# One core, three transformer blocks: the instruction scheduler is given a finer model of the engines

## The chip, the cores and the metric

The kernel runs on one core of one Trainium2 chip. The metric is the device time of one execution in microseconds (us); the kernel before takes 1453.17 us, the median of 3 runs. A core has a matrix engine (PE in the profile, with its weight loads as PEld), a vector engine (DVE), a scalar engine with function tables (ACT), GpSimd (POOL) and SyncE (SP), which issues the DMAs here. Each engine works through its own list of instructions strictly in the order in which the program put them there, and waits on semaphores for the others.

## The reference, cut to what matters

A sequence of 256 tokens of width 1024, in fp32, goes through two layers of a first block and one layer of a second block.

```python
def first_block(x, ...):                       # DEPTH = 2 layers
    h = rms_norm(x, norm1_g[l]); z = h @ w_in[l]
    o_a = mla_mixer(cq, ckv, kpe, ...)         # 8 heads, causal softmax attention
    o_b = gla_mixer(gq, gk, gv, glr, gr, ...)  # gated linear attention in chunks of 64
    o_c = s5_mixer(su, ...)                    # state-space scan
    g = sigmoid(gates + gate_b[l])             # three gates of width 1024
    merged = g0*(o_a @ w_br_mla[l]) + g1*(o_b @ w_br_gla[l]) + g2*(o_c @ w_br_s5[l])
    x = x + merged @ w_out[l]
    x = x + square(relu(rms_norm(x, norm2_g[l]) @ w_ff1[l])) @ w_ff2[l]

def second_block(x, ...):                      # one layer
    z = rms_norm(x, g_pre_mix) @ w_in
    y_attn = dilated_attention_mixer(q, k, v, rel_bias_table, w_attn_out)   # 24 heads in 3 groups
    y_conv = silu(layer_norm(conv31(u * sigmoid(gate)))) @ w_conv_out + b_conv_out
    merged = sigmoid(z_ga)*y_attn + sigmoid(z_gc)*y_conv
    x = x + rms_norm(merged @ w_mix_out, g_post_mix)
    x = x + rms_norm(swiglu_ffn(rms_norm(x, g_pre_ffn), ...), g_post_ffn)
```

## The kernel before, in words

All weights are read once from HBM, in 424 "units" of 128 rows by 1024 columns. For each unit SP issues a DMA into a buffer `raw`; ACT rounds it to the high part `wH` (line 160 of a helper) and DVE forms the rest `wL` (line 161). Each product is made of three matmuls, high by high, low by high and high by low: lines 169, 170 and 171 where the weights are held in the engine and 256 tokens stream past (24 matmuls for a unit), lines 175 to 177 where 512 weight columns stream past the tokens.

The mixers between the weight products are "chains": generators that emit some small PE instructions, then vector and scalar work on their results, and yield. Two chains matter most below. `mla_attn` takes two heads at a time: transposes of q and k into PSUM (line 872), the copy `mla_T` on ACT (875), scores (884, 885), mask and row minimum on DVE (888, 890), exponentials on ACT (895), normalization on DVE (897, 899) into `mla_p`, transposes (906) with their copies `mla_pT` (908), the product with v (912), and the split of the result into `moH` and `moL`, which the product with `w_br_mla` reads. `conv_ln`, the layer norm behind the convolution, sums channels (1346), centres (1359), squares on ACT (1363), sums again (1349), forms the reciprocal root on POOL, broadcasts it over the partitions with two matmuls of a diagonal `diag` (1332, 1333), multiplies (`cv`, 1375; each of two instructions takes four of eight channel blocks), applies SiLU with gain and bias (1378, eight instructions), and splits into `cH` and `cL`, which the product with `w_conv_out` (1551 to 1553) reads. `attn2`, the dilated attention of the second block, has scores (1422, 1424), bias and minimum (1426, 1428), exponentials (1436), scaling (1440), transposes (1448, copied by 1450) and the product with v (1457).

Which unit follows which, and after which unit a chain advances by a step, is written out by hand in the strings `SCHED` (one for each layer) and `SCHED2`; letters with numbers are units, the others are steps of chains. So the program is emitted in one order. Tile, the framework that it is written in, does not keep that order: when the context closes, its scheduler goes through the emitted instructions with a model of the five engines, and on each engine puts next what is ready earliest by that model and by the priorities that the program sets. What it decides is the order of the lists, and these are then fixed; on the chip nothing is reordered.

Buffers are limited: two PSUM buffers for weight products (`ps_mm`), five for chains (`ps_acc`) and one for transposes (`ps_tr`), three `raw` buffers, and four pairs of `wH` and `wL`, fetched three units ahead.

## Time and profile before

| | before |
|---|---|
| median of 3 runs | 1453.17 us (1452.96 to 1453.4) |
| profiled execution, its own time | 1451.78 us |
| its span (first to last instruction) | 1450.0 us |
| PE busy | 1402.2 us, 97% |
| PEld busy | 1272.1 us, 88% |
| DVE busy | 1012.9 us, 70% |
| ACT busy | 835.1 us, 58% |
| mean granted PE clock | 0.991 of full speed |

The profiled execution is 1.39 us under the median, and 1.78 us of it lie outside the span. A busy PE is not a PE at its peak: its matmuls are pipelined and their recorded ends overlap. The time in which PE is idle is what another order can give or take, since the instructions are the same.

### The profile page before, as it was taken

Reading aid. Unit: us, or ns where it says so; the run is one execution under the profiler, and the core shown is the slowest. Engines: PE = TensorE matmul, PEld = TensorE weight load, DVE = VectorE, ACT = ScalarE, POOL = GpSimd, SP = SyncE. Lnnn points to the kernel's source line nnn. Section 1 sums busy time; section 2 is a strip of 40 time slices with the busy share of each in tenths; the row PEclk is TensorE's granted clock in tenths of the full one; section 3 lists DMA queues with packets and bytes.
Section 4 is the critical chain, followed back from the end, with each engine's and each line's share of the span. In section 5 each row is a group of like instructions: output and inputs, shape, how many; then the busy total and the mean of one; then the engine's idle time right before and its main releaser. Section 6 shows DMA issues by size and latency. Waiting matters only on the chain.

```text
span 1450.0 us, 26147 instructions
## 1 busy us (share of the span) xinstructions
PE 1402.2 (97%) x10412; PEld 1272.1 (88%) x10412; DVE 1012.9 (70%) x1860; ACT 835.1 (58%) x1455; POOL 46.3 (3%) x51
## 2 busy tenths in 40 slices
PE   8999999999999999989999999999999999899998
PEld 6989889888899899888988999989888989689997
DVE  6987776689455667766566555579999846655555
ACT  6865566467754555455546444465678574544443
POOL 1000100000000000111000000000000000000000
PEclk9999999999999999999999999999999999999999
DMA  6622344555445552344456555565555445365553
GB/s 221 218 88 90 119 169 151 175 189 177 159 172 185 201 175 77 116 147 160 148 188 225 186 185 189 189 227 183 181 152 171 150 153 183 117 218 189 185 183 112
DMA packets 71058, 243.10 MB, mean 168 GB/s; under 512 B 7864, under 2 KB 11656, under 8 KB 70936
## 3 DMA queue, kind: packets, MB, share of 16 engines
q1 hardware_dynamic: 70936, 241.43, 48.8%
q8 instruction: 81, 1.33, 0.4%
q14 instruction: 41, 0.34, 0.1%
HBM read 237.17 MB, written 4.23 MB: 166 GB/s over the span
## 4 chain that ended last, share of the span: by engine, by line
PE 62%; DVE 13%; ACT 7%; issue 3%; DMA 2%; POOL 2%; POOLq 0%; DVEq 0%; ACTq 0%; SPq 0%
PE mm L169 11%; PE mm L171 11%; PE mm L170 11%; PE acc L175 7%; PE acc L177 7%; PE acc L176 7%; DVE wL L161 4%; ACT wH L160 2%; DVE cv L1321 2%; POOL rsq L184 2%; DMA raw<-in_wst_dram 2%; ACT sp L1436 1%; PE acc L553 1%; PE acc L1457 1%; ACT sp L1440 1%
## 5 line engine op out<-in xcount | busy, mean ns | idle before, releaser
L161 DVE TENSOR_TENSOR wL<-raw,wH 128x1024 fp32r<-128x1024 f32 (+1 forms) x410 | 496.1, 1211 | 260.4 <-ACT wH L160 259.0
L160 ACT ACTIVATE wH<-raw 128x1024 fp32r<-128x1024 f32 (+1 forms) x410 | 429.1, 1048 | 379.5 <-PE mm L170 184.7
L169 PE MATMUL mm<-hH,wH 128*128 128x256 f32 x1792 | 515.5, 288 | 5.0 <-ACT gt L1065 3.5
L171 PE MATMUL mm<-hH,wL 128*128 128x256 f32 x1792 | 510.4, 285 | 0.0
L170 PE MATMUL mm<-hL,wH 128*128 128x256 f32 x1792 | 509.7, 284 | 0.0
L169 PEld LDWEIGHTS mm<-hH,wH 128*128 128x128 f32 x1792 | 342.8, 191 | 17.2 <-issue 4.4
L170 PEld LDWEIGHTS mm<-hL,wH 128*128 128x128 f32 x1792 | 343.2, 191 | 3.6 <-issue 0.4
L171 PEld LDWEIGHTS mm<-hH,wL 128*128 128x128 f32 x1792 | 342.9, 191 | 1.4 <-issue 0.9
L175 PE MATMUL acc<-wH,fH 128*128 128x512 f32 x344 | 135.2, 393 | 0.0
L176 PE MATMUL acc<-wL,fH 128*128 128x512 f32 x344 | 134.8, 392 | 0.0
L177 PE MATMUL acc<-wH,fL 128*128 128x512 f32 x344 | 134.2, 390 | 0.6 <-DVE fL L161 0.6
L1321 DVE SCALAR_TENSOR_TENSOR cv<-u,ppt,cv 128x256 f32<-128x256 f32 x184 | 78.0, 478 | 0.3
L177 PEld LDWEIGHTS acc<-wH,fL 128*128 128x128 f32 x344 | 64.6, 188 | 15.2 <-DVE fL L161 1.1
L175 PEld LDWEIGHTS acc<-wH,fH 128*128 128x128 f32 x344 | 64.9, 189 | 11.4 <-ACT fH L160 0.2
L176 PEld LDWEIGHTS acc<-wL,fH 128*128 128x128 f32 x344 | 64.9, 189 | 10.5
L160 ACT ACTIVATE fH<-ffr 128x256 fp32r<-128x256 f32 x56 | 23.4, 417 | 68.4 <-DVE ffr L1224 68.4
L161 DVE TENSOR_TENSOR fL<-ffr,fH 128x256 fp32r<-128x256 f32 x56 | 23.7, 424 | 23.0 <-ACT fH L160 23.0
L176 PE MATMUL acc<-wL,hH 128*128 128x512 f32 x96 | 37.9, 398 | 0.9 <-DVE wL L161 0.9
L175 PE MATMUL acc<-wH,mH 128*128 128x512 f32 x96 | 37.8, 394 | 0.0
L176 PE MATMUL acc<-wL,mH 128*128 128x512 f32 x96 | 37.8, 394 | 0.0
L175 PE MATMUL acc<-wH,hH 128*128 128x512 f32 x96 | 37.8, 399 | 0.0
L177 PE MATMUL acc<-wH,hL 128*128 128x512 f32 x96 | 37.7, 396 | 0.0
(435 smaller groups left out, 2171.3 us busy)
## 6 DMA issues: line engine op xcount, KB each, us to landing
raw<-in_wst_dram SPq DMA_DIRECT2D x420, 512.0 KB, 3.5
xd<-x SPq DMA_DIRECT2D x6, 512.0 KB, 4.0
x<-xd SPq DMA_DIRECT2D x6, 512.0 KB, 5.7
bias<-bdram SPq DMA_DIRECT2D x8, 384.0 KB, 6.2
gnorm<-in_rows_dram SPq DMA_DIRECT2D x3, 512.0 KB, 5.3
raw<-in_wst_dram SPq DMA_DIRECT2D x4, 384.0 KB, 3.5
x<-in_x_dram SPq DMA_DIRECT2D x4, 256.0 KB, 4.5
x<-in_x_dram SPq DMA_DIRECT2D x2, 512.0 KB, 5.2
```

What stands on the lines that cost most here:

```text
L160: nc.scalar.activation(H, src, AF.Copy)
L161: nc.vector.tensor_sub(L, src, H)
L169: nc.tensor.matmul(ps, H[:, w], aH[:, i, :], start=(i == 0), stop=False)
L170: nc.tensor.matmul(ps, H[:, w], aL[:, i, :], start=False, stop=False)
L171: nc.tensor.matmul(ps, L[:, w], aH[:, i, :], start=False, stop=(i == nk - 1))
L175: nc.tensor.matmul(ps, aH[:, ki, tt], H[:, cols], start=start, stop=False)
L176: nc.tensor.matmul(ps, aH[:, ki, tt], L[:, cols], start=False, stop=False)
L177: nc.tensor.matmul(ps, aL[:, ki, tt], H[:, cols], start=False, stop=stop)
L184: nc.gpsimd.tensor_tensor(o, m, k.mhalf[:, 0:1].to_broadcast([P, n]), op=OP.pow)
L553: nc.tensor.matmul(ps[:, (4 * c + q) * 64:(4 * c + q + 1) * 64], E[:, c, :], us[:, q, :], start=True, stop=True)
L1321: nc.vector.scalar_tensor_tensor(st.cv[:, ct], u(ct, i), w(ct, i), st.cv[:, ct], op0=OP.mult, op1=OP.add)
L1436: nc.scalar.activation(s[i][:, :, cs], s[i][:, :, cs], AF.Exp, scale=-1.0, bias=mj[:, b:b + 1], accum_out=sm[:, b:b + 1])
```

## The change

One argument of the Tile context is set. The scheduler then times the instructions by a finer model of the engines (one that steps through a time line of each instruction's parts) in place of the plain one. The text of the kernel, its hand-written strings and its priorities stay, and so do the instructions: 9582 on PE, 1862 on DVE, 1357 on ACT, 56 on POOL and 484 on SP before and after, with 14 loads of a function table on ACT in both.

```diff
-    with _tile.TileContext(nc) as tc:
+    with _tile.TileContext(nc, schedule_with_timeline_sim=True) as tc:
```

What moves is the place of the instructions in the lists: 5693 of the 9582 on PE, 1451 on DVE and 995 on ACT stand elsewhere, 2 on POOL and 67 on SP. Three places follow. Numbers behind a name tell its allocations apart.

PE at the end of the layer-0 `mla_attn`, its last two heads, before: `tr_3025` are the k transposes, `acc_3164` and `acc_3212` the scores of the two heads, `tr_3226` and `tr_3232` the transposes of their probabilities, and every `mm` is a weight product of 24 matmuls.

```order
L872 MATMUL tr_3025<-cst_85,mla_kn_2854 96x128
...
L171 MATMUL mm_3136<-s5oH_2241,wL_3035 128x256
L884 MATMUL acc_3164<-mla_T_3030,mla_T_3023 128x128
L885 MATMUL acc_3164<-mla_T_3030,mla_T_3023 128x256
L169 MATMUL mm_3184<-hH_187,wH_3066 128x256
...
L171 MATMUL mm_3184<-hH_187,wL_3067 128x256
L884 MATMUL acc_3212<-mla_T_3030,mla_T_3023 128x128
L885 MATMUL acc_3212<-mla_T_3030,mla_T_3023 128x256
L906 MATMUL tr_3226<-cst_85,mla_p_3171 128x128 x3
L169 MATMUL mm_3250<-hH_187,wH_3099 128x256
...
L906 MATMUL tr_3232<-cst_85,mla_p_3219 128x128
```

The same place of the changed kernel:

```order
L872 MATMUL tr_3025<-cst_85,mla_kn_2854 96x128
L884 MATMUL acc_3164<-mla_T_3030,mla_T_3023 128x128
L885 MATMUL acc_3164<-mla_T_3030,mla_T_3023 128x256
L884 MATMUL acc_3212<-mla_T_3030,mla_T_3023 128x128
L885 MATMUL acc_3212<-mla_T_3030,mla_T_3023 128x256
L906 MATMUL tr_3226<-cst_85,mla_p_3171 128x128 x3
L906 MATMUL tr_3232<-cst_85,mla_p_3219 128x128 x3
L912 MATMUL acc_3163<-mla_pT_3230,mla_v_2016 64x256
L912 MATMUL acc_3163<-mla_pT_3236,mla_v_2016 64x256
L912 MATMUL acc_3163<-mla_pT_3230,mla_v_2016 64x128
L912 MATMUL acc_3163<-mla_pT_3236,mla_v_2016 64x128
L169 MATMUL mm_3314<-moH_2017,wH_3180 128x256
```

Weight products of gates and of the S5 branch, three of them ahead of `acc_3164` and one ahead of `acc_3212`, have moved ahead of `tr_3025`, so that the steps of the chain now follow each other directly, up to the product that reads `moH`.

PE between the second broadcast of `conv_ln` (`acc_13455`) and the first product with `w_conv_out` (`mm_13691`), before; `mm_13486` to `mm_13605` are four weight products of the gates, `tr_13555` to `tr_13652` transposes of `attn2`:

```order
L1333 MATMUL acc_13455<-diag_13459,cst_85 128x128
L1424 MATMUL acc_13462<-k_12888,q_12775 128x256
L1424 MATMUL acc_13463<-k_12888,q_12775 128x256
L169 MATMUL mm_13486<-hH_10720,wH_13336 128x256
...
L171 MATMUL mm_13605<-hH_10720,wL_13483 128x256
L1457 MATMUL acc_13554<-pT2_13559,v2_0_10887 64x256
...
L1448 MATMUL tr_13646<-cst_85,sp_13320 128x128 x3
L1448 MATMUL tr_13652<-cst_85,sp_13324 128x128 x3
L1551 MATMUL mm_13691<-cH_13635,wH_13523 128x256
```

And of the changed kernel:

```order
L171 MATMUL mm_13605<-hH_10720,wL_13483 128x256
L1333 MATMUL acc_13455<-diag_13456,cst_85 128x128
L1422 MATMUL acc_13462<-k_12888,q_12775 128x128
L1422 MATMUL acc_13463<-k_12888,q_12775 128x128
L1424 MATMUL acc_13462<-k_12888,q_12775 128x256
L1424 MATMUL acc_13463<-k_12888,q_12775 128x256
L1333 MATMUL acc_13455<-diag_13459,cst_85 128x128
L1551 MATMUL mm_13691<-cH_13635,wH_13523 128x256
L1551 MATMUL mm_13725<-cH_13635,wH_13569 128x256
L1448 MATMUL tr_13555<-cst_85,sp_13320 128x128
L1552 MATMUL mm_13691<-cL_13637,wH_13523 128x256
```

The four gate products now stand ahead of the broadcast, and the transposes of `attn2` behind the first rows of the product with `w_conv_out`.

ACT at the same place, before; the rows on `cv` are SiLU, those of line 1436 exponentials, of 1440 the scaling of `attn2`:

```order
L1378 ACT_TABLE_LOAD
L1378 ACTIVATE cv_11475<-cv_11475,ppt_86 128x256
L1436 ACT_TABLE_LOAD
L1436 ACTIVATE sp_13320,asm_13474<-sp_13320,amj_13472 128x3x128
...
L1378 ACT_TABLE_LOAD
L1378 ACTIVATE cv_11475<-cv_11475,ppt_86 128x256
L1517 ACTIVATE z_13365<-mm_13605 128x256
L1378 ACTIVATE cv_11475<-cv_11475,ppt_86 128x256 x2
L1450 ACTIVATE pT2_13650<-tr_13646 128x3x128
L160 ACTIVATE cH_13635<-cv_11475 128x1024
```

And of the changed kernel:

```order
L1517 ACTIVATE z_13365<-mm_13605 128x256
L1378 ACT_TABLE_LOAD
L1378 ACTIVATE cv_11475<-cv_11475,ppt_86 128x256 x6
L1436 ACT_TABLE_LOAD
L1436 ACTIVATE sp_13320,asm_13474<-sp_13320,amj_13472 128x3x128
L1436 ACTIVATE sp_13320,asm_13474<-sp_13320,amj_13472 128x3x256
L1436 ACTIVATE sp_13324,asm_13515<-sp_13324,amj_13513 128x3x128
L1436 ACTIVATE sp_13324,asm_13515<-sp_13324,amj_13513 128x3x256
L1378 ACT_TABLE_LOAD
L1378 ACTIVATE cv_11475<-cv_11475,ppt_86 128x256 x2
L160 ACTIVATE cH_13635<-cv_11475 128x1024
L1440 ACTIVATE sp_13320<-sp_13320,asm_13474 128x3x128
```

Six SiLU instructions now run in one go, then the table is changed for all four exponentials and back for the last two SiLU, and `cH_13635` stands behind these; the weight splits and copies that stood in between have gone ahead.

## Rows read from the trace of the kernel before

**Rows 1.** The page's part on busy time of each engine.

```profile
PE 1402.2 (97%) x10412; PEld 1272.1 (88%) x10412; DVE 1012.9 (70%) x1860; ACT 835.1 (58%) x1455; POOL 46.3 (3%) x51
```

**Rows 2.** Waits of PE, whole span: us in total, times, longest us.

```profile
PE mm L240 <- DMA x<-in_x_dram: 4.6, 1, 4.6
...
PE mm L169 <- ACT gt L1065: 3.5, 2, 1.8
PE tr L478 <- ACT ET L480: 3.1, 4, 1.4
PE tr L906 <- DVE mla_p L899: 2.4, 2, 1.6
...
PE tr L759 <- DVE gla_og L754: 1.9, 2, 1.0
...
PE tr L478 <- ACT s5ep L463: 1.8, 2, 1.6
...
PE acc L553 <- ACT s5us L548: 1.2, 3, 0.6
...
PE mm L170 <- DVE s5oL L164: 1.1, 2, 0.8
```

**Rows 3.** Busy time in stretches: start:end length, engines (count), then PEclk, DMA share, GB/s.

```profile
236.00:265.00 29.00, 28.99 (x238) 27.59 (x234) 16.14 (x30) 16.29 (x30) 0.00 (x0) 1.00 0.42 146
1146.00:1188.00 42.00, 38.93 (x289) 33.80 (x287) 23.91 (x50) 31.67 (x52) 0.71 (x1) 0.92 0.31 104
1171.00:1179.40 8.40, 5.67 (x46) 4.78 (x45) 3.68 (x3) 8.37 (x16) 0.00 (x0) 1.00 0.48 162
1179.41:1186.23 6.82, 6.66 (x31) 5.33 (x31) 2.16 (x2) 5.30 (x10) 0.00 (x0) 0.50 0.09 34
172.00:182.00 10.00, 7.46 (x61) 7.01 (x61) 8.13 (x18) 6.80 (x12) 3.88 (x2) 1.00 0.18 61
```

**Rows 4.** Timeline of PE, conv_ln: start us, duration us, instruction, idle before and releaser.

```profile
1161.52 0.49 PE L1333 MATMUL acc<-diag,cst 128*128 128x128 f32 x2
...
1180.19 0.80 PE L1551 MATMUL mm<-cH,wH 128*128 128x256 f32 x2 [0.16 <-ACT cH L160]
```

**Rows 5.** Timeline of DVE at the same place.

```profile
1163.19 0.28 DVE L1426 CUSTOM_DVE_ANT_0 sp<-acc,bias 128x128 f32<-128x128 f32 x1
...
1164.30 0.08 DVE L1428 DVE_READ_ACCUMULATOR2_ANT amn<- 128x1 f32 x1
...
1165.57 1.21 DVE L1375 TENSOR_TENSOR cv<-cv,acc 128x1024 f32<-128x1024 f32 x1
...
1180.17 1.23 DVE L161 TENSOR_TENSOR cL<-cv,cH 128x1024 fp32r<-128x1024 f32 x1 [3.26 <-ACT cH L160]
```

**Rows 6.** Timeline of ACT at the same place.

```profile
1164.14 1.28 ACT L1436 ACT_TABLE_LOAD   x1
1165.43 0.62 ACT L1436 ACTIVATE sp<-sp,amj 128x384 f32<-128x384 f32 x1
...
1166.97 0.36 ACT L1517 ACTIVATE z<-mm 128x256 f32<-128x256 f32 x1
...
1167.83 1.43 ACT L1440 ACTIVATE sp<-sp,asm 128x384 f32<-128x384 f32 x2
...
1177.73 1.08 ACT L1378 ACTIVATE cv<-cv,ppt 128x256 f32<-128x256 f32 x2
...
1179.09 1.05 ACT L160 ACTIVATE cH<-cv 128x1024 fp32r<-128x1024 f32 x1
```

**Rows 7.** Timeline of PE, the layer-0 attention tail.

```profile
250.58 0.39 PE L884 MATMUL acc<-mla_T 96*128 96x128 f32 x2
...
253.76 0.30 PE L906 MATMUL tr<-cst,mla_p 128*128 128x128 f32 x1
```

**Rows 8.** Timeline of ACT, the layer-0 attention tail.

```profile
238.85 0.67 ACT L875 ACTIVATE mla_T<-tr,ppt 96x512 f32<-96x512 f32 x1
...
256.05 0.37 ACT L160 ACTIVATE moH<-acc 128x256 fp32r<-128x256 f32 x1
```

## The prediction

> **What bounds the kernel now.** I read the busy times first. PE is busy for 1402.2 of 1450.0 us [rows 1], so it sets the time, and all that another order of the same instructions can take away is its idle 47.8 us, plus what a reduced PE clock costs. Next come the waits of PE, to see where this idle time lies [rows 2]: 4.6 us at the start for the first input, which no order helps, and then many waits of one to two microseconds for a step of a chain, on ACT (`gt`, `ET`, `s5ep`, `s5us`) or on DVE (`mla_p`, `gla_og`, `s5oL`). No single one is large. Then I read stretches [rows 3], to learn how full PE is at the two places where the order changes most. In the layer-0 attention tail (236 to 265 us) PE is busy for 28.99 of 29.00 us: it has nothing to win there. Around the end of `conv_ln` (1146 to 1188 us) it is busy for 38.93 of 42.00, with ACT busy for 31.67. In that stretch lies a half-clock piece: from 1179.41 to 1186.23 us the granted clock is 0.50, the lower of its two levels (1.2 against 2.4 GHz), which costs half of 6.82, or 3.4 us; it follows 8.40 us in which PE was busy for only 5.67. After 10.00 us with 7.46 busy (172 to 182) the clock stayed at 1.00.
>
> Last come the timelines at the two places, for the length of each chain's steps [rows 4 to 8].
>
> **What the change does.** No instruction is added or removed, and the DMAs stand nearly as before, so every term below is idle time of PE that appears or goes. The rule that I use: a step of a chain costs PE nothing as long as the PE rows between the step that feeds it and the step that needs it last longer than the work on DVE and ACT in between. Where those rows have gone, all of that work is exposed.
>
> *The end of `conv_ln`.* Before, four gate products and transposes stand between the second broadcast and the first product with `w_conv_out`; on the trace they span 1161.52 to 1180.19 us, 18.67 us, and at its end PE waits for `cH` by 0.16 us only [rows 4]. After, nothing but that broadcast is ahead of the product. I count from the broadcast, T. DVE has the score reductions in front (1163.19 to 1164.38, 1.2 us; 0.2 for the handoff), then `cv` at 1.2: T+2.6 [rows 5]. ACT does four SiLU on it and two more on the second `cv`, 0.54 each, 1.08 for two [rows 6]: T+5.8. Then come the exponential table, 1.28 and a start 1.29 us later (T+7.1), the four exponentials, 1.54 for each head's two (1165.43 to 1166.97; T+10.2), the SiLU table again (T+11.4), two SiLU (T+12.5) and `cH`, 1.05: **T+13.5**. PE then needs `cL` 1.23 us later and has two matmuls in hand: 1.0 more. The second half, `cH` and `cL`, stands on ACT behind four scalings, 1.43 for two: T+13.5+2.7+1.05 = T+17.2, and its `cL` at T+18.4, while the first half's 22 matmuls last until T+17.4 (0.12 us each, as the 238 PE instructions in the full 28.99 us of 236 to 265 [rows 3]): 1.0 more. Sum 15.5 us of idle PE, against 3.07 in this stretch today (42.00−38.93): **+12.4**. The half-clock piece is there already, so it isn't added. Bounds: +10.4, if ACT is given a step earlier than I think and half of the last two waits vanish, and +13.4, if a weight split stands in the way once more.
>
> One rule of the Trainium skill speaks on the price of the table changes. The trace has the first exponential 1.29 us after its table load began [rows 6], so a change of table costs just the load. The page ScalarE: Activation LUTs, section What ACT_TABLE_LOAD costs, gives the load at about 1283 ns, which agrees, and adds a drain of some 1380 ns. By the page the two changes in the way would add about 2.8 us, an estimate from its figure; by the row they add nothing, and the sum goes by the row.
>
> *The attention tail of layer 0.* Before, three weight products stand ahead of the first scores and one ahead of the second; PE waits for nothing. After, each step follows the last. Waits: `mla_T`, 0.67 [rows 8] and handoffs, 0.9; from scores to normalized `mla_p` 3.18 us (250.58 to 253.76 [rows 7]), less the second head's scores and handoff, 2.6; the second head's exponentials behind the first's, and one PSUM buffer for both heads' transposes with a copy between, of about 0.5 us (between those of `mla_T` and `moH` in size), 0.8; the second copy, 0.5; `moH` 0.37 [rows 8] and then `moL`, of about the same size, 0.7. **+5.5** us; +4.3, if the second head overlaps entirely, to +8, if two splits of 1.2 us (the rows of `cL` and `cv` show that size) stand in the way.
>
> *The layer-1 tail* has the same chain, but gate products stay between its scores and transposes; only the copy, `moH` and `moL` are bare: **+2** (1.1 to 3.5).
>
> *Other exposed steps.* Some S5, gated-attention and transpose steps, and handoffs at phase ends, stand closer to their feeders by a fraction of a microsecond each; ten or so at about half of one: **+5** (0 to 8; the nearest rows, `s5us` 1.2 for three and `s5oL` 1.1 for two [rows 2], are of that size each).
>
> *Waits that go.* Through layers 0 and 1 most chain steps stand later in PE's list by 5 to 15 us worth of weight matmuls. Of the waits listed I take `mla_p` 2.4, `gla_og` 1.9, `s5ep` 1.8, `s5us` 1.2 and `s5oL` 1.1 as covered, 8.4 us. `gt` 3.5 and `ET` 3.1 stay: these are copies out of PSUM buffers that PE wants again, of which there are as few as before. Of what is left in smaller waits, 47.8−4.6−3.1−15.0 = 25.1, I take a quarter, 6.6. **−15.** Bounds: −8 (the listed ones alone) to −25 (those and two thirds of the rest).
>
> *Clock.* A stall of 5 us in the attention tail is longer than what preceded the half-clock piece at 1179; such a piece costs 3.4 us when it is 6.8 us long, and today's trace also has shorter stalls that brought none. I take **+1.7** (−1.7, if one of today's goes instead, to +5).
>
> Sum: 12.4+5.5+2+5−15+1.7 = +11.6 us. On the profiled execution's 1451.78 that gives 1463.4. That execution is 1.39 us under the median, so on the median's scale it is **1464.8**. All lower bounds together give −11, all upper ones +30, but they are not likely to fall together.
>
> **The rivals.**
>
> *The waits go, and more than the tails cost* (faster). The mechanism: the chain steps that stand later in PE's list cover the small waits of both layers, not only the listed ones. For it speaks that these are many and that PE's step is the only one that has moved far. Against it: at two places the list leaves PE nothing to do, and that is seen in the rows, not guessed. Its price: −25 against 12.4+5.5 at the two tails and nothing elsewhere: −7, or **1446**. It decides when the waits that go exceed 18 us.
>
> *Nothing to gain or lose* (same). PE's work is the same and fills 97% of the span; an order moves its idle time and doesn't change it: the two tails cost 18, the waits that go give back 18. **1453**. For it speaks that today's waits are spread over the whole span, so that one freed in front is often met again behind. The Trainium skill's page Perfetto Trace Analysis, section Identifying the Most-Contended Engine, would have one judge PE by the share of its weight loads, 88% here [rows 1]; by that rule PE remains the bound whatever the order is, and a change that leaves its instructions alone gives no change. The trace agrees with the share, but the idle time that the order exposes isn't in it.
>
> *A larger loss* (slower). The stalls in both tails, in the layer-1 tail and at one S5 step are each followed by a half-clock piece of 6.8 us, two or three more than today, and of the waits only the listed 8 us go: 12.4+5.5+3.5+6+6.8−8 = +26, or **1479**. For it: the piece at 1179 followed 2.7 us of idle time; against it: 172 to 182 us had 2.5 us idle without one.
>
> **How the numbers follow.** Forecast as summed, 1457 to 1472: 0.53. Larger loss: 0.18. Faster: 0.17. Same: 0.12. Change of the order without effect isn't a case of its own: the lists differ. About 0.2% (2.9 us) is what a measurement of this kernel tells from no change. So slower has 0.71, same 0.12, faster 0.17. The likeliest alone has 1457 to 1472; the range for 8 in 10 reaches into the faster case and the larger loss, 1448 to 1477.
>
> **What would show it.** In the changed kernel's profile: PE idle for some 13 us ahead of line 1551, with `cH` on ACT as releaser, and about 15 us idle in that stretch; a chain of short PE stalls at lines 884, 906, 912 and at the first product with `moH` near 255 us, some 5 us together; smaller entries for `mla_p`, `gla_og` and `s5ep` in the list of waits, and unchanged ones for `gt` and `ET`; PE idle in all near 58 us against 47.8; table loads on ACT still at 1.28. I am wrong if the wait ahead of line 1551 is under 5 us, which would mean that ACT's list runs ahead of what I count, or if the waits that go exceed 18 us.

## The result and the profile after

| | before | changed |
|---|---|---|
| median | 1453.29 us (4 runs, 1452.96 to 1455.04) | 1519.10 us (4 runs, 1515.28 to 1521.67) |
| profiled execution, its span | 1451.78 us, 1450.0 us | 1518.62 us, 1516.8 us |
| mean granted PE clock | 0.991 | 0.971 |

The ratio is 1.0448, 95% interval 1.0424 to 1.0472. The changed kernel is slower by 66 us where the forecast had 11.6: the direction was right, the size was not, and the time lies outside the range.

First the page, for the sum. Busy time of each engine in the changed kernel, and the granted clock in 40 slices:

```profile
PE 1420.6 (94%) x10412; PEld 1289.6 (85%) x10412; DVE 1009.1 (67%) x1860; ACT 833.9 (55%) x1455; POOL 39.3 (3%) x51
...
PEclk9989989999999999999999999999999979999999
```

Against [rows 1], PE has the same 10412 rows of matmuls but is busy 18.4 us longer, and its idle time is 1516.8−1420.6 = 96.2 us against 47.8: 48.4 more. Together that is the 66.8 us by which the span grew. DVE and ACT are not busier. Every slice of the clock line was a 9 before; now three are below.

Then where it arises. The transposes of the norms (line 240) open each layer's FFN and the next layer in both kernels, so their starts mark the same point of the work. Rows of that line in three stretches, with first and last start; before:

```profile
L240 PE MATMUL mm<-cst,x x8: 270/272/329, 485.0 to 489.7; 128*128 128x128 f32 x8
...
L240 PE MATMUL mm<-cst,x x8: 272/273/328, 757.8 to 762.1; 128*128 128x128 f32 x8
...
L240 PE MATMUL mm<-cst,x x8: 270/272/328, 941.1 to 945.7; 128*128 128x128 f32 x8
```

and changed:

```profile
L240 PE MATMUL mm<-cst,x x8: 272/273/329, 515.0 to 516.7; 128*128 128x128 f32 x8
...
L240 PE MATMUL mm<-cst,x x8: 270/273/273, 799.7 to 800.9; 128*128 128x128 f32 x8
...
L240 PE MATMUL mm<-cst,x x8: 272/272/330, 987.5 to 989.2; 128*128 128x128 f32 x8
```

The lag is 30.0 us at the start of layer 1, 41.9 at its FFN and 46.4 at the start of the second block; at the last such row (1251.4 before, 1316.5 after) it is 65.1. The stretches that hold mixers lose (30, with layer 0's FFN in it, then 12 and 19 us), the one with layer 1's FFN 4.5. So the loss is spread over the whole program, and about two thirds of it lie in the two layers to which the forecast gave little.

Last, what PE waits for. The waits of the changed kernel, whole span: us in total, times, longest us.

```profile
PE mm L1551 <- ACT cH L160: 13.4, 1, 13.4
PE tr L872 <- ACT mla_T L875: 7.2, 2, 6.3
PE tr L759 <- DVE gla_og L754: 5.6, 1, 5.6
...
PE mm L169 <- DVE hL L161: 3.3, 1, 3.3
PE mm L171 <- DVE wL L161: 3.3, 5, 1.0
PE acc L175 <- ACT hH L163: 3.1, 4, 1.2
PE tr L240 <- DVE rL L161: 3.0, 2, 2.2
PE acc L175 <- ACT rH L160: 2.6, 4, 1.0
...
PE tr L478 <- ACT s5ep L463: 1.9, 1, 1.9
...
PE mm L169 <- ACT gt L1065: 1.8, 3, 1.0
PE tr L906 <- DVE mla_p L899: 1.6, 2, 1.4
...
PE acc L553 <- ACT s5us L548: 1.1, 2, 0.6
```

The row of `mla_T` was this before:

```profile
PE tr L872 <- ACT mla_T L875: 1.8, 2, 1.0
```

All waits in this view sum to 87.2 us, before to 40.7. Of the 46.5 more, 13.2 are the end of `conv_ln` (13.4 against 0.2). The splits of the activations that are transposed at the norms (`hH`, `hL`, `rH`, `rL`), which before cost 0.2 us in all, make 12.0; `mla_T` grew by 5.4 and `gla_og` by 3.7 [rows 2 has its 1.9]; the splits of weights (`wL`, `wH`) grew from 1.9 to 7.2. These five make 39.4; the rest is small steps.

### The profile page after: what moved, and what is told of

Same layout as the page of the kernel before. It is cut to its first block, busy times and chain, and to the rows that moved or that the text cites. A ratio compares the mean times of both kernels' runs of the same rounds, so it can differ in the third digit from the quotient of the medians.

```text
span 1516.8 us, 26182 instructions
## 1 busy us (share of the span) xinstructions
PE 1420.6 (94%) x10412; PEld 1289.6 (85%) x10412; DVE 1009.1 (67%) x1860; ACT 833.9 (55%) x1455; POOL 39.3 (3%) x51
## 4 chain that ended last, share of the span: by engine, by line
PE 56%; ACT 4%; DVE 3%; DMA 1%; issue 1%; POOL 0%; SPq 0%; DVEq 0%; POOLq 0%; ACTq 0%
PE mm L169 11%; PE mm L171 10%; PE mm L170 10%; PE acc L175 6%; PE acc L176 6%; PE acc L177 6%; DVE wL L161 1%; ACT wH L160 1%; DMA raw<-in_wst_dram 1%; ACT sp L1436 1%; PE acc L1457 1%; PE mm L1552 1%; PE tr L1448 1%; PE mm L1553 1%; PE mm L1551 1%
## 5 line engine op out<-in xcount | busy, mean ns | idle before, releaser
L169 PE MATMUL mm<-hH,wH 128*128 128x256 f32 x1792 | 514.6, 287 | 13.5 <-DVE hL L161 3.3
L175 PE MATMUL acc<-wH,fH 128*128 128x512 f32 x344 | 131.3, 393 | 0.4 <-ACT fH L160 0.4
L177 PE MATMUL acc<-wH,fL 128*128 128x512 f32 x344 | 130.0, 390 | 0.0
L177 PEld LDWEIGHTS acc<-wH,fL 128*128 128x128 f32 x344 | 64.5, 188 | 13.5
L175 PEld LDWEIGHTS acc<-wH,fH 128*128 128x128 f32 x344 | 64.6, 189 | 12.1 <-ACT fH L160 0.8
L164 DVE SCALAR_TENSOR_TENSOR wL<-raw,ppt,wH 128x512 fp32r<-128x512 f32 x40 | 28.3, 746 | 14.2 <-ACT wH L163 14.2
L163 ACT ACTIVATE wH<-raw,ppt 128x512 fp32r<-128x512 f32 x40 | 26.5, 715 | 19.0 <-PE acc L177 9.1
```

Source lines behind the costliest of these rows:

```text
L163: nc.scalar.activation(H, src, AF.Copy, scale=scale)
L164: nc.vector.scalar_tensor_tensor(L, src, scale, H.bitcast(F32), op0=OP.mult, op1=OP.subtract)
L169: nc.tensor.matmul(ps, H[:, w], aH[:, i, :], start=(i == 0), stop=False)
L175: nc.tensor.matmul(ps, aH[:, ki, tt], H[:, cols], start=start, stop=False)
L177: nc.tensor.matmul(ps, aL[:, ki, tt], H[:, cols], start=False, stop=stop)
```

## Two waits, read to their cause

`gla_og`, the largest wait in layer 1. The timelines of ACT and DVE at that place (start us, duration us, instruction, idle before and releaser; the row of ACT is the first of four):

```profile
660.15 0.28 ACT L747 ACTIVATE gla_sq<-acc 128x128 f32<-128x128 f32 x1
...
661.72 0.23 DVE L854 TENSOR_SCALAR krc<-rsq,mla_rs 128x4 f32<-128x4 f32 x1 [1.12 <-POOL rsq L184]
...
662.40 0.16 DVE L748 TENSOR_SCALAR gss<-gss 128x4 f32<-128x4 f32 x1
663.75 0.23 DVE L750 TENSOR_SCALAR rsq<-rsq,rsn 128x4 f32<-128x4 f32 x1 [1.19 <-POOL rsq L184]
664.01 1.13 DVE L754 SCALAR_TENSOR_TENSOR gla_og<-acc,rsq,sr 128x128 f32<-128x128 f32 x4
```

PE runs out of work at 658.77 and starts line 759 at 664.41. The sums of squares that line 748 needs have had their input since 635.40, but ACT's list has other steps in front of them, and they run from 660.15 to 661.29. DVE could go on with them, but has line 854 in front, a step of the MLA branch's k, and that waits 1.12 us for POOL; line 748 starts at 662.40, 1.1 us late. So a ready step stands behind another branch's step that isn't ready. Then come POOL's own root, 1.0, and the four products, 1.13. All of this is bare, since no weight product stands ahead of line 759 on PE's list any more: the kernel before has these squares 22.5 us behind their input too (601.40 to 623.92), but PE had products left to run and waited 0.90 us.

`mla_T`, the largest in layer 0. The timeline of ACT:

```profile
197.65 1.06 ACT L620 ACTIVATE s5w<-s5y 128x1024 f32<-128x1024 f32 x1
200.73 1.06 ACT L623 ACTIVATE s5w<-s5w 128x1024 f32<-128x1024 f32 x1 [2.02 <-DVE s5w L622]
201.69 0.67 ACT L875 ACTIVATE mla_T<-tr,ppt 96x512 f32<-96x512 f32 x1
```

PE's transposes of q ended at 196.12, so the copy was ready to run from then on. It stands behind the S5 chain's line 623, which waits 2.02 us for DVE and runs 1.06, and behind five short or ready steps before that. PE waits 6.30 us, of which 5.57 pass before the copy starts. In both places each engine's list is in order, and the steps of two branches are interleaved so that one's wait becomes the other's; that makes most of the wait for `mla_T`, and a smaller part of that for `gla_og`, where the missing cover on PE weighs more.

## The experiments

Three helpers occur. *Pinning* hands the scheduler a stored list, and lets each instruction of an engine follow the one before it on that list; it fixes order and adds no wait on the chip:

```diff
...
+    for a, b in zip(names, names[1:]):
+        tc.add_manual_dep(by[b], a, NoSync)
```

*Holding* makes the first matmul of a weight product follow a named chain step on PE's list, in the same way. The others are edits of the strings that order the units, and in e12 added matmuls. Ratios are against the kernel before in the same set of runs.

**Whole lists (e1 to e4).** The same two lines, with another choice of lists each time:

```diff
+        _pin(tc, nc, _ORDERS)     # e1: PE; e2: ACT, DVE, POOL, SP; e3: all, both layers; e4: all
```

> PE's list is put back to that of before, instruction by instruction; the finer model still orders ACT, DVE, POOL and SP around it. Theory A (the loss comes from PE's list, where chain steps stand without weight products between them): within 10 us of before, 1453 to 1463, PE idle near 48 us. Theory B (the loss comes from the lists of DVE and ACT, where the step of one chain stands behind the waiting step of another): most of the loss stays, 1490 to 1520. Theory C (a third of the loss is PE's reduced clock, which follows its stalls) goes with A here: half-clock pieces as few as before.

> The lists of ACT, DVE, POOL and SP are put back to those of before; the finer model orders PE alone, around them. Theory A: over 1485, since PE's list is still the finer model's own. Theory B: 1453 to 1465, since no step stands behind another chain's any more.

> All five lists are put back for the two layers of the first block; the finer model orders the second block alone. By the trace of the changed kernel 43 to 50 of its 65 us have arisen when the second block begins. If the loss stands where the trace shows it: 1470 to 1476, with the wait of about 13 us ahead of line 1551 still there. If stalls only move on to the next phase, as a rival has it: over 1490.

> All five lists are put back to those of before, with the option still set. If the order is all that the option changes: 1453, within 2 us. If the option changes something else as well (waits, buffers): different by more.

| | median us | ratio, 95% interval |
|---|---|---|
| e1, PE's list of before, other lists by the finer model | 1533.39 | 1.0564 [1.0540, 1.0589] |
| e2, the other lists of before, PE's by the finer model | 1564.23 | 1.0771 [1.0743, 1.0799] |
| e3, all lists of before in both layers, second block by the finer model | 1475.27 | 1.0167 [1.0139, 1.0195] |
| e4, all lists of before | 1451.18 | 0.9993 [0.9979, 1.0006] |

e4 shows that the option acts through the order alone: with the old order the time is the old one. e3 shows that the loss adds up by place: the two layers alone carry 0.0281 of the 0.0448, some 41 us, and the second block the other 24. e1 lies outside both of its forecasts, and e2 comes out as theory A has it, which e1 had refuted. Every account that looks at one engine's list alone misses, mine too: with PE's list put back, the kernel is slower than the changed one, and so it is with all the others put back. One place of e1 shows how. PE waits there as its old list wants the transposes of `attn2` next (timelines of PE and of ACT in e1):

```profile
1250.98 0.48 PE L1448 MATMUL tr<-cst,sp 128*128 128x128 f32 x1 [8.09 <-ACT sp L1440]
...
1240.80 2.06 ACT L1378 ACTIVATE cv<-cv,ppt 128x256 f32<-128x256 f32 x4
1242.77 1.04 ACT L160 ACTIVATE cH<-cv 128x1024 fp32r<-128x1024 f32 x1
1243.83 1.28 ACT L1436 ACT_TABLE_LOAD   x1
...
1250.33 2.76 ACT L1440 ACTIVATE sp<-sp,asm 128x384 f32<-128x384 f32 x4
```

ACT's list takes all eight SiLU, which are ready, and `cH`, before the exponentials that PE's list needs first. At this place the lists of the two engines do not agree on which chain goes first, and PE pays.

**Holding PE's list at the two predicted places (e5, e6).** The gate products may not go ahead of the second broadcast of `conv_ln`; in e6 none may go ahead of each step of `mla_attn`:

```diff
...
+            if i == 0 and k.hold is not None:
+                tc.add_manual_dep(m0.ins, k.hold.ins.name, NoSync)
...
+    k.hold = k.last            # e5: behind the second broadcast
+        k.hold = last          # e6: behind each PE step of mla_attn
```

> The changed kernel with one rule added: the four gate products that the program emits behind the second broadcast of the layer norm may not stand ahead of it in PE's list. Theory G (the finer model uses up ready products while a chain works, and leaves none for the chain's last steps): the wait of 13.4 us ahead of the first product with cH falls below 3 us, the half-clock piece of 17 us there shrinks, and the time falls by 10 to 16 us, to 1503 to 1509. Rival: the stall moves to the broadcast itself or behind, and the time stays over 1515.

> The changed kernel with the same rule for both layers' mla_attn: weight products emitted behind its k transposes, scores or probability transposes may not stand ahead of them. Theory G: the bare tail of layer 0 is covered again, about 6 us idle and 3 us of clock less there, and somewhat less in layer 1: 1503 to 1513. Rival (a rule on PE alone moves stalls, as with PE's list put back, since ACT and DVE are ordered by the same model): 1519 or more.

e5 gave 1521.25 us, 1.0497 [1.0476, 1.0518]. The wait ahead of the product with `w_conv_out` is gone, as the edit intended, but the time isn't back. The waits of PE in e5 (its line numbers are two to six higher):

```profile
PE mm L171 <- ACT z L1523: 6.2, 2, 4.9
...
PE mm L171 <- ACT g2th L1501: 2.8, 1, 2.8
...
PE acc L1337 <- DVE diag L1336: 2.6, 2, 1.4
```

The gate products stand where they stood before, but the scheduler's ACT list has their copies (`z`, `g2th`) behind other steps, and PE waits for PSUM buffers. These three are 11.6 us, against 4.1 in the changed kernel, and PE is busy for 1425.5 us against 1420.6, at a mean clock of 0.968 against 0.971. So 7.5 of the 13.4 us are seen to come back there; where the rest went was not read. e6 gave 1563.14 us, 1.0778 [1.0762, 1.0794]: `mla_T` 12.9, `gla_og` 12.5 and `mla_p` 11.7 in its waits. So the theory that the moved weight products alone are at fault at these two places, and that holding PE's list there undoes the loss, falls.

**Is it the strings (e7, e8)?** The hand-written strings could fit the plain model's order and no other. Their steps were shuffled by a few places, the same way for both models; e7 is the plain model, e8 the finer one:

```diff
-    "su0 kg s s s su2 s su1 su3 gk0 s gq0 s gq1 s s cq0 gk1 l s cq2 ...
+    "su0 kg s su2 s s su1 su3 s s gk0 s s gq0 gq1 s cq0 l gk1 s cq2 ...
```

> The kernel before, under the plain model, with its hand-written strings shuffled at random by a few places (chain steps against units; no unit changes its place among units). Theory F (the strings are fitted to the order that the plain model makes of them; any other order loses): 15 to 60 us slower than before, 1468 to 1513. Theory Q (the finer model's orders are worse in themselves): within 10 us of before.

> The same shuffled strings under the finer model. Theory F: within 15 us of the changed kernel and of the shuffled plain one, 1490 to 1530. Theory Q: 50 us or more above the shuffled plain one.

e7: 1460.62 us, 1.0085 [1.0060, 1.0111], 10.4 us above the kernel before of its set, just outside theory Q and below theory F. e8: 1522.42 us, 1.0501 [1.0485, 1.0516]. The plain model loses 0.0085 to the shuffle, the finer one 0.0053 more than without it. The gap between the models stays at 0.0416 against 0.0448, 61.8 us here, as theory Q has it. So the loss isn't a misfit of these strings; the finer model's choice of order is worse for both that were tried.

**The mirror of e1 and e2 (e9, e10).** The plain model, with PE's list of the changed kernel (e9) or with its other lists (e10):

```diff
+        _pin(tc, nc, _ORDERS)     # e9: PE of the changed kernel; e10: ACT, DVE, POOL, SP of it
```

> The plain model again, with PE's list alone taken over from the changed kernel; the plain model orders the other engines around it. Theory S (a list that is made by what is ready now puts chain steps late, and each list carries that loss by itself): 1510 to 1560, as bad as the changed kernel or worse. Rival (only the finer model's way with ACT and DVE is bad, and PE's list could be lived with): under 1475.

> The counterpart: the lists of ACT, DVE, POOL and SP taken over from the changed kernel, PE ordered by the plain model around them. Theory S: 1510 or more. Rival (PE's list alone carries the loss): under 1475.

e9: 1518.13 us, 1.0451 [1.0427, 1.0476], the same as the changed kernel. e10: 1583.64 us, 1.0910 [1.0872, 1.0949]. Either half of the changed lists is enough to carry the whole loss, and neither half of the old lists (e1, e2) to undo it. The wait for `cH` ahead of line 1551 is there in both, 12.1 us in e9 and 13.3 in e10. In all four mixtures the lists that are not pinned are made anew around the pinned ones, so they are neither those of before nor those of the changed kernel. That pinning by itself spoils them can be excluded: with its own PE list pinned, or its own other four, either model makes the remaining lists as it does without (this is read from the programs as built, not from a run).

**Is it lateness alone (e11)?** In the changed kernel the chains run later: the products of the layer-0 and layer-1 probabilities with v (line 912) have their first and last start at 190.2 and 722.1 us before, and at 217.9 and 766.5 after. So the plain model was given strings in which each chain step stands behind up to two of the units that followed it:

```diff
-    "su0 kg s s s su2 s su1 su3 gk0 s gq0 s gq1 s s cq0 gk1 ...
+    "su0 kg su2 su1 s s s su3 s gk0 gq0 gq1 s cq0 s gk1 s s ...
```

> The kernel before, plain model, with each chain step of the hand-written strings moved behind up to two following units, 24 to 48 of PE's matmuls, about as far as the changed kernel puts PE's chain steps later (64 rows behind where they are emitted, against 20 before). If lateness of the chains alone makes the loss: 30 us or more slower than before. If the loss needs the step-by-step disorder between the lists, and chains that are late as a whole do little harm: within 20 us of before.

1466.83 us, 1.0102 [1.0076, 1.0129]: chains that are later by this much cost 0.0102, some 15 us. But the shift is smaller than was meant: in e11 the starts of line 912 are 200.5 and 740.1, so 10.3 and 18.0 us later than before, where the changed kernel has 27.7 and 44.4. So e11 shows that lateness costs something; how much of the loss it makes at the changed kernel's size stays open.

**The clock (e12).** Behind the broadcast, where the changed kernel's PE waits 13.4 us, 96 needless matmuls run; the product that follows overwrites their result, so the output is the same.

```diff
...
+            if n == 4:
+                for i in range(96):
+                    m = nc.tensor.matmul(ps[:, :S], H[:, 0:P], st.hH[:, 0, :], start=True, stop=True)
...
```

> The changed kernel with 96 needless matmuls (11.5 us at 0.12 each), whose result is overwritten, in the wait of 13.4 us ahead of the first product with cH; all lists stay otherwise. If the half-clock piece there comes from PE's idleness: the granted clock stays at 1.00 behind the wait and the stretch from the broadcast to the end of the next 60 us is 3 to 4 us shorter, although PE does more. If the clock falls for another reason: no change there, within 1 us.

The same stretch in windows (length, then PE, PEld, DVE, ACT and POOL busy, PEclk, DMA share, GB/s), changed kernel first, then e12:

```profile
1230.36:1247.43 17.07, 6.46 (x28) 6.13 (x29) 3.48 (x7) 14.36 (x25) 0.00 (x0) 0.50 0.14 56
```

```profile
1230.00:1247.00 17.00, 14.70 (x118) 13.48 (x117) 3.75 (x5) 15.01 (x25) 0.00 (x0) 1.00 0.06 22
```

The half-clock piece is gone, and the product with `cH` starts as late as it did: 13.86 us behind the broadcast, 13.85 without the edit. So at this place the piece follows PE's idleness, and busy work in the gap prevents it. From the broadcast to the next transposes of line 240, changed kernel first:

```profile
1226.87:1309.49 82.62, 68.24 (x454) 62.09 (x453) 42.22 (x62) 45.69 (x70) 0.55 (x1) 0.90 0.41 140
```

```profile
1224.71:1305.15 80.44, 77.38 (x551) 70.97 (x550) 42.31 (x62) 45.62 (x70) 0.55 (x1) 1.00 0.43 144
```

The stretch is 2.2 us shorter, although PE does more in it; 3 to 4 had been forecast. The whole span is 5.0 us shorter, but the rest of that lies outside the edit's stretch. The median of two runs was 1515.73 us, 1.0432 [1.0398, 1.0466]; that overlaps the changed kernel's interval, so a gain of the whole kernel is not shown.

**Single places in the old order, all five lists (e13, e14).** In e13 the rows put back run from the middle of the second block's convolution to the first product with `w_attn_out`, which take in all of `conv_ln` and some of the products with `w_conv_out` but none with `w_mix_out`; in e14 they are those of the layer-0 mixers:

```diff
+        _pin(tc, nc, _ORDERS)     # e13: mid-convolution to w_attn_out; e14: the mixers of layer 0
```

> The changed kernel, with the rows of all five lists from the middle of the second block's convolution to the products with w_mix_out put back among themselves to their order of before; the rest is the finer model's. If the loss sits in the lists of one place and is additive: the 12 us that arise there by the trace go, with 3 us of half-clock counted in them, 1504 to 1510, and no long wait ahead of line 1551. Rival (the stall moves on as it did when only PE's list was held there, 1521): 1515 or more.

> The changed kernel, with the rows of all five lists of layer 0's mixers (up to the product with w_out) put back to their order of before. By the trace 24 to 26 us arise there. Additive: 1491 to 1498. Rival (the stalls move on into the feed-forward part): 1510 or more.

e14: 1495.99 us, 1.0319 [1.0301, 1.0336]; 0.0129 of the 0.0448 comes back, some 19 us, from one layer's mixers, as the additive account has it; `mla_T` is gone from the front of its list of waits, while `gla_og` of layer 1 stays at 5.6. e13: 1512.52 us, 1.0432 [1.0412, 1.0453], between its two forecasts; the intervals do not tell it from the changed kernel. (Its time is 6.6 us lower, but the kernel before was 3.6 lower in that set as well.) Its waits of PE:

```profile
PE tr L1448 <- ACT pT L1450: 5.1, 2, 3.4
...
PE mm L169 <- ACT g2th L1495: 3.4, 1, 3.4
```

The 13.4 us ahead of line 1551 are gone, and these two are 8.5 us where the changed kernel has 1.3 (it doesn't wait for `pT`), so that 7.2 have come back around the pinned piece. So with all lists together a layer's mixers can be repaired (e14, e3); at the shorter place of e13 no gain is clear of the noise.

## Why the prediction was right in its sign and wrong in its size

**The end of `conv_ln`: right.** The timeline of PE, changed kernel:

```profile
1226.87 0.49 PE L1333 MATMUL acc<-diag,cst 128*128 128x128 f32 x2
1240.72 0.79 PE L1551 MATMUL mm<-cH,wH 128*128 128x256 f32 x2 [13.36 <-ACT cH L160]
...
1241.98 0.58 PE L1552 MATMUL mm<-cL,wH 128*128 128x256 f32 x1 [0.25 <-DVE cL L161]
```

From the broadcast to the product are 13.85 us where the count gave 13.5. The wait for `cL` is 0.25, not 1.0: a transpose of `attn2` stands between, which the count left out, and at half clock it and the two matmuls last longer (at full clock, in e12, the wait is 0.42). The second 1.0, for the other half's `cL`, does not appear. So PE is idle for 13.6 us there against the 15.5 counted, which is +10.5, just above the lower bound of 10.4. On ACT the steps came in the order that was counted:

```profile
1232.88 1.28 ACT L1436 ACT_TABLE_LOAD   x1
1234.18 0.61 ACT L1436 ACTIVATE sp<-sp,amj 128x384 f32<-128x384 f32 x1
...
1237.34 1.28 ACT L1378 ACT_TABLE_LOAD   x1
1238.63 1.09 ACT L1378 ACTIVATE cv<-cv,ppt 128x256 f32<-128x256 f32 x2
1239.63 1.04 ACT L160 ACTIVATE cH<-cv 128x1024 fp32r<-128x1024 f32 x1
```

Each table load is followed by its first instruction 1.30 and 1.29 us after it began, here with the load on PE's path. The row's price holds; the drain that the Trainium skill adds (ScalarE: Activation LUTs, What ACT_TABLE_LOAD costs) isn't seen in this place.

**The layer-0 attention tail: the right stalls, smaller than counted.** They came at the lines named:

```profile
276.55 0.49 PE L884 MATMUL acc<-mla_T 96*128 96x128 f32 x2 [0.77 <-ACT mla_T L875]
...
279.55 0.61 PE L906 MATMUL tr<-cst,mla_p 128*128 128x128 f32 x3 [1.43 <-DVE mla_p L899]
280.74 0.55 PE L906 MATMUL tr<-cst,mla_p 128*128 128x128 f32 x3 [0.58 <-ACT mla_pT L908]
281.87 1.55 PE L912 MATMUL acc<-mla_pT,mla_v 128*64 128x256 f32 x8 [0.58 <-ACT mla_pT L908]
283.90 0.80 PE L169 MATMUL mm<-moH,wH 128*128 128x256 f32 x2 [0.48 <-ACT moH L160]
```

They sum to 3.84 us, where 5.5 were forecast and 4.3 was the lower bound; PE is idle for 4.47 of the 26.00 us around them, but that takes in 0.62 for `gt` ahead of the tail. The term most too large was the one for `mla_p`, 2.6 against 1.43. **The layer-1 tail** has waits of 0.16 for `mla_p`, 0.58 for its copy and 0.48 for `moH`: 1.2, within its 1.1 to 3.5.

**Waits that go, −15: the step that failed first.** I took chain steps that stand later in PE's list to be covered by the weight products that now stand ahead of them. Of the five waits listed, 8.4 us together [rows 2], two went as counted: `s5oL` has no row left, and the 1.6 that `mla_p` still has are the 1.43 and 0.16 of the two tails. But `s5ep` and `s5us` are met again elsewhere with 1.9 and 1.1 (1.8 and 1.2 before), and `gla_og` rose from 1.9 to 5.6: together 8.6 us, so that nothing was gained where 8.4 were to go. (The other 6.6 were a guess, and a quarter of 25.1 is 6.3.) The rule failed because it looked at PE's list alone and took what moves later there for covered. PE's products moved as well, so that none is left ahead of `gla_og`, and on ACT and DVE a step can stand behind another branch's waiting step, as the two timelines show. Nor did `gt` and `ET` stay as they were: `gt` fell from 3.5 to 1.8, and `ET`, with 3.1 before, is now met at three lines for 4.9.

**Other exposed steps, +5 (0 to 8): the step that failed most.** With the conv wait and the two tails taken out of the 46.5 us by which the waits grew, 46.5−13.2−3.8−1.2 leaves some 28, where this term and the last gave −10. I had looked at the three places that the order shows at a glance, and counted the others as fractions of a microsecond. The splits at the norms alone are 12.0, and I had no term for them. Before layer 1, products of the FFN filled the time between the transposes of `x` and the first product that reads them (the eight transposes shown start over 4.7 us); now the transposes come in 1.7 us, the product follows at once, and PE waits 0.34 and 0.97 us there. The largest single one is 3.3 us for `hL`.

**The clock, +1.7: off by a factor of ten.** PE has the same instructions and is busy 18.4 us longer. I priced one half-clock piece. There are 13 in the changed kernel and 5 before, mostly where the waits bunch, and the longest is 17 us. The windows of the changed kernel at the layer-0 tail and of the piece behind `gla_og` (columns as above):

```profile
262.00:288.00 26.00, 21.53 (x144) 18.43 (x144) 10.14 (x35) 12.22 (x31) 0.00 (x0) 0.87 0.23 82
...
663.75:670.58 6.83, 5.08 (x22) 4.54 (x23) 3.44 (x10) 2.59 (x6) 0.00 (x0) 0.50 0.01 3
```

Windows laid on all pieces at 0.50 have these sums and means of length and busy time, the kernel before first:

```profile
sum 24.82, PE 17.73 PEld 15.41 DVE 12.80 ACT 13.31 POOL 1.54; mean PE 3.55 PEld 3.08 DVE 2.56 ACT 2.66 POOL 0.31
```

```profile
sum 88.51, PE 61.38 PEld 54.28 DVE 40.33 ACT 42.09 POOL 4.74; mean PE 4.72 PEld 4.18 DVE 3.10 ACT 3.24 POOL 0.36
```

The pieces are 64 us longer. What they cost is seen in PE's busy time inside them, 61.4 us against 17.7: half of the 43.7 between is 21.9, an estimate, near the 18.4 by which the busy time grew. The Trainium skill (TensorE: Matmul & The Clock Gate, HAM oscillation) counts a throttled stretch at half of its time, by which 64 us would be 32, an estimate; that is too much here, since PE stands idle in part of those pieces, as for 10.6 of the 17.07 us above. That longest piece costs no more than what the kernel before has at the same place: PE is busy for 6.46 us in it, and for 6.66 in the shorter one there [rows 3]. So the added cost comes from the other pieces, such as the one behind `gla_og`.

**The rivals.** Faster and same are out: what went (`s5oL`, `mla_p` outside the tails, and `pT` with 1.9) is far less than what came. The larger loss had the right mechanism, stalls that each bring a half-clock piece while only few waits go, and too few places: its 1479 is 40 us short. The rule on the most-contended engine (the Trainium skill, Perfetto Trace Analysis, Identifying the Most-Contended Engine), which judges PE by the share of its weight loads, was read in the prediction as no change; that share stayed above those of DVE and ACT (85%) while the span grew by 66.8.

**What stays open.** Shown: only the order acts (e4); the loss is in the main a sum over places (e3, e14); part of the lists from one model and the rest from the other gain nothing (e1, e2, e9, e10); it isn't the strings (e8). Lateness of the chains costs something (e11), but was not tried at its full size. Why the finer model's choices give worse lists is argued, not shown. At the three places read here it puts on each engine what is ready, ahead of what another engine's list needs next, and every mismatch is paid by PE, which has no slack. No run changed the scheduler's rule itself, and no version tried beats the kernel before: e4 has its time.

## What to carry to other kernels

Where one engine is busy for 97% of the span, a change of order has 3% to win and much more to lose, so price it by how many places lose their cover and not by the two or three that the order shows at a glance. A lost cover is paid as a wait and, where a half-clock piece follows in which PE is busy, once more: here 48.4 us of idle time and 18.4 of longer busy time. A chain step that moves later on one engine is covered only if its feeders on the other engines haven't moved behind another chain's waiting step, so the lists of all engines have to be read together. And a list that works is a set: half of it, mixed with another order, was slower than either whole in three of the four mixtures.

## What the runs showed of the hardware that I had not expected

The granted clock stayed at 0.50 for 17.07 us in one piece, and PE was busy 18.4 us longer with the same instructions, in a kernel whose PE was still busy for 94% of its span; the pieces at 0.50 hold 61.4 us of its busy time, against 17.7 before. With 96 needless matmuls in a 13.4 us gap, PE kept its full clock (1.00 against 0.50), the matmuls behind the gap started 0.12 us apart in place of 0.21, and the stretch up to the next transposes was 2.2 us shorter with more work in it.
